# Softmax-sum spreading by transposition, one norm accumulator per half, and last products over two tiles, in a hybrid attention and FFN block

## The chip, the cores and the metric

The kernel runs on one core of a Trainium2 chip. The metric is device microseconds of one execution. It took 1214.15 us before the change, the median of 3 runs between 1213.70 and 1214.68. Less is better.

## The reference

One layer over 1024 frames of width 1024, in fp32: an RMS norm, one combined projection, two groups of eight heads (softmax attention in a band, group A; stick-breaking attention, group B), an RMS norm of each group, one output projection with residual, an RMS norm, a gated FFN with a causal convolution of width 3 and residual, and a last RMS norm.

```
h = rmsnorm(x, norm1_g);  qa, ka, va, qb, kb, vb = split(h @ w_in)
ya = chunked_attention(qa, ka, va, rel_bias)   # p = softmax(qk/8 + bias), band of 9 chunks of 64
yb = stick_breaking_attention(qb, kb, vb)
x = x + concat(rmsnorm(ya, norm_a_g), rmsnorm(yb, norm_b_g)) @ w_out
u = conv3(rmsnorm(x, norm2_g) @ w_ffn_in) + conv_b;  gate, val = split(u)   # 2816 each
x = x + (silu(gate) * val) @ w_ffn_out
return rmsnorm(x, final_g)
```

## The kernel before

**Layout.** Activations lie transposed: a tile holds 128 features on the partitions and frames along the row, and `x2` is eight such tiles. A half is 512 frames (index `g`), a block is 128 frames. Products with full precision are split in high and low parts, three matmuls (fp32r) for one product; the softmax work, the transpositions and the sums of norms are plain fp32, and one such matmul may show as several records in the trace.

**Stages**, by time in the trace: projections to about 200 us; group B's attention to 341; group A's attention, 341 to 498; group A's part of the output projection (`pa`, eight feature tiles d for half 0 and then half 1), 510 to 559; with it, and into the first FFN products, the second norm; the FFN's up-projection with convolution, to about 990; its down-projection, to 1177; the last products (`last_down`) with the final norm and the output, to the end.

**Group A.** Four pairs of heads p, eight blocks i of 128 queries each. Of a block and head (h = 0, 1), TensorE makes the scores `sa` (L1058, L1059); VectorE adds the bias and takes the row maximum (L1074, L1077); ScalarE makes the exponentials `pa` with their row sums (L1086), which lie in columns 2 and 3 of the small tile `st` (`sta` in the trace); VectorE writes the reciprocals to columns 4 and 5 (`self.scale`). `turn` has TensorE transpose `pa` (`tpa`, L1111) and ScalarE copy the result to `pta` (L1115). `spread` (L1121) brings the reciprocals into the layout of the output: 64 rows of the PSUM bank `yy` hold the reciprocal sums of head 0, 64 those of head 1, for 128 queries along the row; it takes two matmuls of a column broadcast to 64 columns with the identity. `output` (L1137) then makes the attention products beside it. Blocks go through `spread` and `output` in pairs, so there are 16 such places. A planner, `flow`, holds an estimate of each engine's clock and puts matmuls of the output projection (`k_p`, `pb`) between this work as filler; `flow.need(x)` fills until x is estimated to be done.

**The second norm.** For a half, `norm_part` has ScalarE square each x2 tile as it is finished; the first square starts an accumulator, those of d = 1 to 6 go through `sq` and an addition on GpSimd (L1680), and that of d = 7 is written straight into a second accumulator (L1674). `totals` (L168) sums the partitions of the accumulators, with four matmuls of two output columns per accumulator, into `n_ms`; a root and a reciprocal follow (L160, L161), the spreading across partitions (`n_rb`, L181), and for each feature tile a multiplication on VectorE (L1699), a copy to the high part on ScalarE, and the low part on VectorE (L129). Half 0's norm is stepped beside half 1's `pa`, a step after each d by `(1, 1, 1, 1, 1, 1, 1, 2)`, the first step being the sums and the root. Half 1's begins in `up_first`, after five products of `up_first` (`plain`, L1919, three matmuls each).

**The end.** `last_down` works on three chunks of columns: frame blocks 0 to 2, 3 to 5, and 6 to 7. For a tile d, TensorE makes the product, VectorE adds it to x2 (L2291), ScalarE squares it (in the last chunk the squares of d = 5, 6, 7 go straight into accumulators of their own, the others through GpSimd). `final` then makes the root, `n_rb`, a copy `n_rbs` of it in SBUF for GpSimd, and the outputs. In the last chunk VectorE makes six outputs with x2, the gain as a scalar and `n_rb` (L2266); for d = 2 and 4 ScalarE has applied the gain ahead (L2295) and GpSimd multiplies with `n_rbs` (L2264). Four DMAs of two tiles each follow on SyncE's queue (L2305).

**Constants.** `cst` is one tile of 216 columns (gains, convolution weights, a bias column), fetched at the start on ScalarE's DMA queue (L116).

## Time and profile before

| What | Value |
|---|---|
| median of 3 runs | 1214.15 us |
| the profiled execution, its own time | 1214.94 us |
| span of the trace in it | 1213.2 us |
| TensorE matmuls busy (PE) | 99% of the span |
| VectorE busy (DVE) | 77% |
| ScalarE busy (ACT) | 56% |
| GpSimd busy (POOL) | 13% |

The span is 1.74 us shorter than the execution that it belongs to, which is what lies around it. In rows of a timeline the columns are the start in us, the duration in us, the engine, the line, the operation, the tiles (out, then in), for PE the size of the weights, the shape and type, and the number of records run together; a last bracket names the wait ahead and who ended it. Matmul records overlap (the next begins before the last has ended), so a rate is read from starts, not from the sum of durations.

### The profile page before, as it was taken

How to read it: one execution, taken by the hardware profiler on the slowest of the kernel's cores; microseconds unless marked ns; L12 is line 12 of the kernel's file. 1: busy time of each engine (PE TensorE's matmuls, PEld its weight loads, DVE VectorE, ACT ScalarE, POOL GpSimd, SP SyncE). 2: the span in 40 equal slices, each digit the busy share in tenths (PEclk: the TensorE clock that was granted, in tenths of full speed). 3: DMA queues.
4: the chain of work that ended last, by engine and by line, in shares of the span. 5: the costliest groups of instructions: out<-in, count | busy, mean ns of one | idle time of the engine just before them, and what ended most of it. 6: DMA issues, size and time to landing. Idle time of an engine off the chain costs nothing.

```text
span 1213.2 us, 17233 instructions
## 1 busy us (share of the span) xinstructions
PE 1195.3 (99%) x6364; PEld 989.3 (82%) x6364; DVE 928.4 (77%) x1385; ACT 676.6 (56%) x1214; POOL 158.9 (13%) x162
## 2 busy tenths in 40 slices
PE   9999999999999999999999999999999999999997
PEld 6788888888878778788878888888888888888887
DVE  7957649878756677459997767777677779969896
ACT  7865336766666566334674555545555455444424
POOL 0001031102211111142000000000000023042036
PEclk9999999999999999999999999999999999999998
DMA  9468677877478841143033122231322196420003
GB/s 333 131 208 267 184 229 206 218 173 197 136 190 249 218 120 57 36 137 124 32 107 105 65 92 84 73 101 59 101 75 82 60 370 264 174 105 1 1 1 139
DMA packets 73650, 166.93 MB, mean 138 GB/s; under 512 B 7639, under 2 KB 23127, under 8 KB 73566
## 3 DMA queue, kind: packets, MB, share of 16 engines
q1 hardware_dynamic: 73422, 165.72, 43.0%
q8 instruction: 50, 0.82, 0.3%
q14 instruction: 34, 0.28, 0.1%
q10 hardware_dynamic: 144, 0.11, 0.0%
HBM read 118.60 MB, written 47.20 MB: 137 GB/s over the span
## 4 chain that ended last, share of the span: by engine, by line
PE 89%; DVE 5%; ACT 2%; DMA 2%; issue 1%; POOL 0%; SPq 0%; DVEq 0%; ACTq 0%; POOLq 0%
PE u_c L1867 9%; PE u_e L1867 9%; PE u_a L1867 9%; PE dz L2366 8%; PE u_b L1867 5%; PE dj L2366 4%; PE dm L2366 4%; PE v_x L503 4%; PE pa L151 3%; PE k_p L151 3%; PE v_y L503 3%; PE yb L1008 3%; PE tpb L994 3%; PE q_p L151 3%; PE yy L1137 2%; PE tpa L1111 2%
## 5 line engine op out<-in xcount | busy, mean ns | idle before, releaser
L967 DVE TENSOR_TENSOR_SCAN acts<-zb,first 128x128 f32<-128x128 f32 (+7 forms) x64 | 86.4, 1351 | 18.5 <-ACT zb L976 18.3
L1891 DVE SCALAR_TENSOR_TENSOR vt<-cv,cst,vt 128x1023 f32<-128x1023 f32 (+1 forms) x44 | 57.3, 1302 | 2.2 <-ACT vt L1885 1.4
L1891 DVE SCALAR_TENSOR_TENSOR gt<-cg,cst,gt 128x1023 f32<-128x1023 f32 (+1 forms) x44 | 56.3, 1281 | 0.9
L1086 ACT ACTIVATE pa<-sa,sta 128x640 f32<-128x640 f32 (+4 forms) x64 | 42.8, 670 | 23.3 <-DVE sta L1077 16.9
L976 ACT ACTIVATE zb<-zb 128x128 f32<-128x128 f32 (+7 forms) x64 | 40.9, 640 | 26.4 <-PE zb L959 26.4
L129 POOL TENSOR_TENSOR dx_0wl<-dr,dx_0wh 128x512 fp32r<-128x512 f32 x1 | 1.5, 1462 | 413.5 <-PE u_b L1867 413.5
L1885 ACT ACTIVATE gt<-cg,cst 128x1024 f32<-128x1024 f32 x22 | 27.4, 1244 | 36.7 <-DVE cg L1759 36.6
L998 ACT COPY tb<-tpb 128x128 f32<-128x128 f32 (+3 forms) x96 | 43.0, 484 | 6.1 <-PE tpb L994 5.3
L1115 ACT COPY pta<-tpa 128x512 f32<-128x512 f32 (+3 forms) x80 | 36.7, 483 | 16.7 <-PE tpa L1111 14.7
L994 PE MATMUL tpb<-ident,acts 128*128 128x128 f32 x288 | 43.2, 277 | 0.0
L1077 DVE TENSOR_REDUCE sta<-sa 128x1 f32<-128x640 f32 (+4 forms) x64 | 41.7, 655 | 1.3
L1756 DVE TENSOR_TENSOR up_r<-up_r 128x512 f32<-128x512 f32 x60 | 41.2, 686 | 0.8
L1111 PE MATMUL tpa<-ident,pa 128*128 128x128 f32 x240 | 38.0, 277 | 1.0 <-ACT pta L1115 0.8
L994 PEld LDWEIGHTS tpb<-ident,acts 128*128 128x128 f32 x288 | 33.1, 140 | 6.3 <-issue 2.6
L1074 DVE TENSOR_TENSOR sa<-sa,bias 128x256 f32<-128x256 f32 (+1 forms) x64 | 26.3, 413 | 12.4 <-PE sa L1059 10.2
L1111 PEld LDWEIGHTS tpa<-ident,pa 128*128 128x128 f32 x240 | 27.9, 140 | 8.1 <-issue 2.6
L2054 ACT COPY u_b<-u_a 128x512 f32<-128x512 f32 x19 | 10.8, 571 | 38.1 <-PE u_a L1867 38.1
L1008 PE MATMUL yb<-tb,dv 128*64 128x128 f32 x448 | 29.2, 273 | 0.0
L151 PE MATMUL pb<-yh,wo_h 128*128 128x512 f32 x64 | 27.3, 426 | 1.7 <-DVE x L1212 1.7
L1756 DVE TENSOR_TENSOR dr<-dr,dr 128x512 f32<-128x512 f32 x40 | 28.8, 740 | 0.0
L1137 PE MATMUL yy<-pta,v 128*64 128x256 f32 (+1 forms) x288 | 28.7, 344 | 0.0
L1900 DVE TENSOR_TENSOR vt<-vt,gt 128x1024 f32<-128x1024 f32 x22 | 26.8, 1218 | 1.2 <-ACT gt L1897 1.1
(1395 smaller groups left out, 4000.8 us busy)
## 6 DMA issues: line engine op xcount, KB each, us to landing
up_r<-in_w_up_dram SPq DMA_DIRECT2D x44, 512.0 KB, 3.6
act<-vt SPq DMA_DIRECT2D x22, 512.0 KB, 2.6
dr<-in_w_dn_dram SPq DMA_DIRECT2D x20, 512.0 KB, 6.8
dr<-act SPq DMA_DIRECT2D x20, 512.0 KB, 6.9
wv<-in_w_v_dram SPq DMA_DIRECT2D x16, 256.0 KB, 5.4
xin<-in_xT_dram SPq DMA_DIRECT2D x16, 256.0 KB, 5.4
row<-in_x_rows_dram SPq DMA_DIRECT2D x16, 256.0 KB, 2.7
raw<-in_w_in_dram SPq DMA_DIRECT2D x8, 512.0 KB, 5.1
```

What stands on the lines that cost most here:

```text
L151: PE.matmul(o, w[:, sl], t[:, rows(g)], start=first and i == 0, stop=last and i == 2,)
L503: PE.matmul(bank[j], t[:, cols(j)], w, start=p in (1, 5) and k == 0 and i == 0, stop=k == 3 and i == 2, skip_group_check=True,)
L967: V.tensor_tensor_scan(out=a[:, :w], data0=z, data1=first[:, :w], initial=1.0, op0=ALU.mult, op1=ALU.max,)
L994: PE.transpose(tp[:, cols(b)], self.a[h][:, cols(b0 + b)], ident)
L998: mine.append(flow.add(on_s(m * P, lambda o=o, tp=tp: S.copy(o, tp))))
L1008: PE.matmul(yy[HS[h], :], (d if j else v)[:, off : off + 64], self.at[h][:, self.c0[h] + j * P : self.c0[h] + (j + 1) * P], start=j == 0, ...
L1111: PE.transpose(tp[:, cols(b)], self.pr[src][:, cols(c)], ident)
L1137: PE.matmul(yy[HS[h], q], v[:, c * P + h * 64 : c * P + (h + 1) * 64], t[:, h], start=j == 0, stop=j == len(parts) - 1, skip_group_check=True,
L1756: eng.tensor_tensor(out=out, in0=a, in1=b, op=ALU.subtract)
L1867: PE.matmul(o, w[:, cols(k)], t, start=start and k == 0 and i == 0, stop=k == 3 and i == 2, skip_group_check=True,)
L1891: V.scalar_tensor_tensor(out=t[:, : T - lag], in0=o[:, lag:], scalar=c1(c + ct), in1=t[:, : T - lag], op0=ALU.mult, op1=ALU.add,)
L2366: PE.matmul(o[m], w[:, cols(m)], t, start=i in (0, 1, 4, 5) and p == ps_[0] and j == 0, stop=p == ps_[-1] and j == 2, skip_group_check=True,)
```

## The change

**Group A.** In `turn` of head 1, ScalarE copies the two reciprocals of a block, each broadcast to 64 columns, to a tile of 128 by 128 (`sh`, one tile of two blocks, one buffer). `spread` transposes that tile into `yy`, one transposition for a block instead of two matmuls, and waits for the copy instead of the reciprocals.

```
-                flow.need(self.scale)
-                for h in range(2):
-                    PE.matmul(
-                        rr[HS[h], :], self.st[:, 4 + h : 5 + h].to_broadcast([P, 64]), ident,
-                        start=True, stop=True, skip_group_check=True,
-                    )
+                o, wide = self.share
+                flow.need(wide)
+                PE.transpose(rr, o.rearrange("p h c -> p (h c)"), ident)
...
+                if h:
+                    if not odd:
+                        shares[self.p] = pools["sbuf"].tile([P, 2, 2, 64], F32, tag="sh", name=f"sh{nm}", bufs=1)
+                    o, share = shares[self.p][:, odd], self.st[:, 4:6].rearrange("p (h c) -> p h c", c=1)
+                    self.share = o, flow.add(
+                        on_s(P, lambda o=o: S.copy(o, share.to_broadcast([P, 2, 64]))), after=[self.scale]
+                    )
```

On TensorE, at the first spread after 350 us (head pair 0, blocks 2 and 3), before:

```order
L1059 MATMUL sa_5_0_4201<-la_3589,qa_3440 128x384
L1121 MATMUL yy_3_4206<-ident,sta_2_0_4024 64x128 x2
L1121 MATMUL yy_3_4206<-ident,sta_3_0_4076 64x128 x2
L1137 MATMUL yy_3_4206<-pta_2_4102,v_2960 64x256 x8
L1137 MATMUL yy_3_4206<-pta_2_4102,v_2960 64x128 x4
L1111 MATMUL tpa_4_0_4233<-ident,pa_4_0_4163 128x128 x4
```

and in the changed kernel:

```order
L1062 MATMUL sa_5_0_4208<-la_3592,qa_3440 128x384
L1131 MATMUL yy_3_4214<-ident,sha_2_4129 128x128 x2
L1144 MATMUL yy_3_4214<-pta_2_4110,v_2960 64x256 x8
L1144 MATMUL yy_3_4214<-pta_2_4110,v_2960 64x128 x4
L1121 MATMUL tpa_4_0_4239<-ident,pa_4_0_4168 128x128 x4
```

Four matmuls with 64 columns of weights have become two with 128, in the same place; the neighbours are the same.

**The second norm.** Each half has one accumulator: the square of d = 7 too goes through `sq` and the addition on GpSimd, and `totals` takes four matmuls instead of eight. Half 0's norm is stepped by `(0, 1, 1, 1, 1, 1, 2, 2)`, one `pa` later, and half 1's sums stand behind six products of `up_first` instead of five.

```
-        accs = {0: [acc0[:, rows(i)] for i in range(2)]}
+        accs = {0: [acc0[:, rows(0)]]}
...
-                accs[1] = [at1[:, rows(i)] for i in range(2)]
+                accs[1] = [at1[:, rows(0)]]
...
-                for _ in range((0, (1, 1, 1, 1, 1, 1, 1, 2)[d])[g]):
+                for _ in range((0, (0, 1, 1, 1, 1, 1, 2, 2)[d])[g]):
...
-                    if n == 5:
+                    if n == 6:
                         next(norms[1])
```

On VectorE, where half 1's last `pa` tiles are added to x (L1208 and L1212, now L1215 and L1219) beside half 0's norm (L1699, now L1706; low parts L129, now L132), before:

```order
L1208 TENSOR_TENSOR pa_1_5711<-pa_1_5711,rba 128x512
L1212 TENSOR_TENSOR x_6_5268<-x_6_5268,pa_1_5711 128x512
L1699 SCALAR_TENSOR_TENSOR x_5_4925<-x_5_4925,cst,n_0_rb 128x512
L129 TENSOR_TENSOR h2l_5707<-x_4_4924,h2h_5706 128x512
L1208 TENSOR_TENSOR pa_1_5735<-pa_1_5735,rba 128x512
L1212 TENSOR_TENSOR x_7_5269<-x_7_5269,pa_1_5735 128x512
L1699 SCALAR_TENSOR_TENSOR x_6_5268<-x_6_5268,cst,n_0_rb 128x512
L129 TENSOR_TENSOR h2l_5731<-x_5_4925,h2h_5730 128x512
L1699 SCALAR_TENSOR_TENSOR x_7_5269<-x_7_5269,cst,n_0_rb 128x512
```

and in the changed kernel:

```order
L1215 TENSOR_TENSOR pa_1_5720<-pa_1_5720,rba 128x512
L1219 TENSOR_TENSOR x_6_5290<-x_6_5290,pa_1_5720 128x512
L1706 SCALAR_TENSOR_TENSOR x_4_4938<-x_4_4938,cst,n_0_rb 128x512
L132 TENSOR_TENSOR h2l_5716<-x_3_4519,h2h_5715 128x512
L1706 SCALAR_TENSOR_TENSOR x_5_4939<-x_5_4939,cst,n_0_rb 128x512
L132 TENSOR_TENSOR h2l_5740<-x_4_4938,h2h_5739 128x512
L1215 TENSOR_TENSOR pa_1_5749<-pa_1_5749,rba 128x512
L1219 TENSOR_TENSOR x_7_5291<-x_7_5291,pa_1_5749 128x512
L1706 SCALAR_TENSOR_TENSOR x_6_5290<-x_6_5290,cst,n_0_rb 128x512
```

Half 0's tile 5 has its norm multiplication two instructions later, and its low part two behind that; the last rows are the same in both.

**The end.** In the last chunk the sums x2 are written into the output tiles `res` (four feature tiles each), ScalarE applies the final gain to all eight, and the last multiplications go over two tiles at a time: three on VectorE (with `n_rb` broadcast over both) and one on GpSimd (tiles 2 and 3), each followed by its DMA.

```
+ENDS = ((0, 0), (4, 0), (2, 1), (6, 0))
...
+                if c_end == KT:
+                    for a, g in ENDS:
+                        y = res[a // 4][:, a % 4 : a % 4 + 2, :]
+                        f = (rb if g else ob).rearrange("p (o t) -> p o t", o=1).to_broadcast([P, 2, n])
+                        (GP if g else V).tensor_tensor(out=y, in0=y, in1=f, op=ALU.mult)
+                        nc.sync.dma_start(outT[a : a + 2, :, sl].rearrange("d p t -> p d t"), y)
+                    return
...
+            def gain(d):
+                y = res[d // 4][:, d % 4, :]
+                S.activation(y, y, AF.Copy, scale=c1(C_GF + d))
...
+                    if c_end == KT:
+                        if d < 4:
+                            gain(d)
```

(The calls of `gain` for d = 4 to 7 stand behind the root in the code; the scheduler puts the instructions where the rows below have them.) On ScalarE, from the root of the second chunk (`n_3_ms`) to that of the last (`n_6_ms`), before:

```order
L160 ACTIVATE rn_78<-n_3_ms,eps 128x3
L2295 ACTIVATE x2n_9047<-x2n_9047,cst 128x256
L2258 COPY n_3_rbs<-n_3_rb 128x384
L1679 ACTIVATE n_sq_10635<-x2n_9048 128x256
L1679 ACTIVATE n_sq_10634<-x2n_9049 128x256
L2295 ACTIVATE x2n_9049<-x2n_9049,cst 128x256
L1674 ACTIVATE n_acc_10629<-x2n_9050 128x256
L1674 ACTIVATE n_acc_10630<-x2n_9051 128x256
L1674 ACTIVATE n_acc_10631<-x2n_9052 128x256
L160 ACTIVATE rn_78<-n_6_ms,eps 128x2
```

and in the changed kernel, from two instructions ahead of the first root and without its last four rows ahead of the second:

```order
L1686 ACTIVATE n_sq_10648<-res_10646 128x256
L2293 ACTIVATE res_10646<-res_10646,cst 128x256
L163 ACTIVATE rn_78<-n_3_ms,eps 128x3
L2293 ACTIVATE res_10646<-res_10646,cst 128x256
L1686 ACTIVATE n_sq_10649<-res_10646 128x256
L2270 COPY n_3_rbs<-n_3_rb 128x384
L2293 ACTIVATE res_10646<-res_10646,cst 128x256
L1686 ACTIVATE n_sq_10648<-res_10647 128x256
L2293 ACTIVATE res_10647<-res_10647,cst 128x256
L1681 ACTIVATE n_acc_10643<-res_10647 128x256
L2293 ACTIVATE res_10647<-res_10647,cst 128x256
L1681 ACTIVATE n_acc_10644<-res_10647 128x256
```

Each square is now followed by a gain of its tile, and two gains stand ahead of the first root.

**Constants.** `cst` holds 40 columns; the 176 columns of the convolution are a tile of their own, fetched on SyncE's queue in `up_first`, behind the weights of up-projection tile 1 and ahead of those of tile 2.

```
-    cst = one("cst", "cst", shape=(P, C_N))
-    nc.scalar.dma_start(cst, consts[:, :C_N])
+    cst = one("cst", "cst", shape=(P, C_W0))
+    nc.scalar.dma_start(cst, consts[:, :C_W0])
...
+            nc.sync.dma_start(conv["t"], consts[:, C_W0:C_N])
             load_up(2)
```

More of the change, by code (lines that the diff above doesn't have):

```diff
@@ L35 @@
 ORDER_B = (7, 0, 6, 1, 5, 2, 4, 3)
-POOL_D = {3: (2,), 6: (6, 7), 8: (2, 4)}
+POOL_D = {3: (2,), 6: (6, 7)}
+ENDS = ((0, 0), (4, 0), (2, 1), (6, 0))
 BACK, BACK_STEP = 1.0, 0.6
@@ L56 @@
 H2_TAGS = {0: ("x6", "x7"), 1: ("x0", "x1"), 2: ("x2", "x3")}
-C_G1, C_G2, C_GY, C_GF, C_W0, C_W1, C_W2, C_CB, C_TB = 0, 8, 16, 24, 32, 76, 120, 164, 208
+C_G1, C_G2, C_GY, C_GF, C_TB, C_W0, C_W1, C_W2, C_CB = 0, 8, 16, 24, 32, 40, 84, 128, 172
 C_N = 216
@@ L113, in one @@
         return pool.tile(list(shape), dt, tag=tag, name=name)
-    cst = one("cst", "cst", shape=(P, C_N))
-    nc.scalar.dma_start(cst, consts[:, :C_N])
+    cst = one("cst", "cst", shape=(P, C_W0))
+    nc.scalar.dma_start(cst, consts[:, :C_W0])
+    conv = {}
     def c1(off):
-        return cst[:, off : off + 1]
+        t, off = (cst, off) if off < C_W0 else (conv["t"], off - C_W0)
+        return t[:, off : off + 1]
     ident = one("ident", "ident", shape=(P, P))
@@ L1142, in output @@
                 flow.work(0.15)
-        pts, x2, yh, yl, yb_of, yq_of, bias_of = {}, {}, {}, {}, {}, {}, {}
+        shares, pts, x2, yh, yl, yb_of, yq_of, bias_of = {}, {}, {}, {}, {}, {}, {}, {}
         rb_of, sq_of, y_chains, x2_chains, yb_chains = {}, {}, {}, {}, {}
@@ L1749, in tile_hybrid_block @@
         fp = pools["sbuf"]
+        conv["t"] = fp.tile([P, C_N - C_W0], F32, tag="conv", name="conv", bufs=1)
         def at(slot, name, dt=F32):
@@ L2252, in final @@
                 rstd([a[:, sl] for a in last], c0, c_end, D, rn2, f"n3_{c0}")
+                if c_end == KT:
+                    for d in range(4, KT):
+                        gain(d)
                 yield
@@ L2258, in final @@
                 S.copy(rb, ob)
+                if c_end == KT:
[5 more added lines that the diff above has]
+                    return
                 pool_d = POOL_D[c_end]
                 for d in range(KT) if c_end == 6 else sorted(range(KT), key=lambda d: d not in pool_d):
-                    x = x2[d][:, sl]
-                    y = res[d // 4][:, d % 4, :] if c_end == KT else x
+                    x = y = x2[d][:, sl]
                     if d in pool_d:
@@ L2268, in final @@
                         )
-                    if c_end < KT:
-                        nc.sync.dma_start(outT[d][:, sl], y)
+                    nc.sync.dma_start(outT[d][:, sl], y)
                     if d not in pool_d:
                         yield
+            def gain(d):
+                y = res[d // 4][:, d % 4, :]
+                S.activation(y, y, AF.Copy, scale=c1(C_GF + d))
             def go(steps):
@@ L2290, in last_down @@
                             )
-                    V.tensor_tensor(out=x2[d][:, sl], in0=x2[d][:, sl], in1=o, op=ALU.add)
+                    y = x2[d][:, sl] if c_end < KT else res[d // 4][:, d % 4, :]
+                    V.tensor_tensor(out=y, in0=x2[d][:, sl], in1=o, op=ALU.add)
                     last = accs[: {3: 1, 6: 2, 8: 4}[c_end]]
-                    x2_part(x2, d, sl, [a[:, sl] for a in last], None, f"n3_{c0}", sqs[d % 2][:, :GW])
-                    if d in POOL_D[c_end]:
+                    x2_part({d: y}, d, slice(0, y.shape[1]), [a[:, sl] for a in last], None, f"n3_{c0}", sqs[d % 2][:, :GW])
+                    if c_end == KT:
+                        if d < 4:
+                            gain(d)
+                    elif d in POOL_D[c_end]:
                         S.activation(x2[d][:, sl], x2[d][:, sl], AF.Copy, scale=c1(C_GF + d))
@@ L2303, in last_down @@
             go(20)
-            for i in range(4):
-                nc.sync.dma_start(
-                    outT[2 * i : 2 * i + 2, :, sl].rearrange("d p t -> p d t"),
-                    res[i // 2][:, 2 * (i % 2) : 2 * (i % 2) + 2, :],
-                )
         done = up_second(up_first())
@@ L2413, in _layout @@
             cols(a("norm1_g")[0]), cols(a("norm2_g")[0]), cols(a("norm_a_g")[0]),
-            cols(a("norm_b_g")[0]), cols(a("final_g")), cols(conv_w[0]), cols(conv_w[1]),
-            cols(conv_w[2]), cols(a("conv_b")[0]), np.broadcast_to(rel[:, -1], (P, 8)),
+            cols(a("norm_b_g")[0]), cols(a("final_g")), np.broadcast_to(rel[:, -1], (P, 8)),
+            cols(conv_w[0]), cols(conv_w[1]), cols(conv_w[2]), cols(a("conv_b")[0]),
             np.zeros((P, GW), np.float32),
```

## The prediction

> **What bounds the kernel.** I read the page's span and engine line first, then its chain, then the waits of TensorE, and only then the three places that the change touches.
>
> ```profile
> span 1213.2 us, 17233 instructions
> PE 1195.3 (99%) x6364; PEld 989.3 (82%) x6364; DVE 928.4 (77%) x1385; ACT 676.6 (56%) x1214; POOL 158.9 (13%) x162
> PE 89%; DVE 5%; ACT 2%; DMA 2%; issue 1%; POOL 0%; SPq 0%; DVEq 0%; ACTq 0%; POOLq 0%
> ```
>
> TensorE is busy for 99% of the span and holds 89% of the chain that ends last. So a matmul taken out is worth its slot unless the next one then waits for its data; and the 11% of the chain on other engines is where a saving can be lost. The waits (engine, line and tile, who released it: us in total, times, the longest) say where PE stands still already in group A, its output projection and the end:
>
> ```profile
> PE na_rb L181 <- DVE rn L1167: 2.2, 1, 2.2
> PE pb L151 <- DVE x L1212: 1.7, 1, 1.7
> PE sa L1058 <- ACT pa L1086: 1.3, 2, 1.2
> PE tpa L1111 <- ACT pta L1115: 0.8, 1, 0.8
> ```
>
> All of these together are 6.0 us. The kernel has little slack to give and little to lose, so the change is a sum of microseconds. The profiled execution took 1214.94 us, of which 1213.2 are the span and 1.74 lie around it; the median of the runs is 0.79 lower, so I apply the sum to the median. A difference of 0.2% (2.4 us) is about what a measurement of this kernel can tell from no change: faster means below 1211.7, slower above 1216.6.
>
> **Group A, what is removed.** The spread's records as a group, then in order of time at one pair of blocks early in the stage and at the last:
>
> ```profile
> L1121 PE MATMUL yy<-ident,sta x128: 272/273/323, 352.1 to 494.7; 128*64 128x128 f32 x128
> 352.14 0.66 PE L1121 MATMUL yy<-ident,sta 128*64 128x128 f32 x8
> 352.63 2.33 PE L1137 MATMUL yy<-pta,v 128*64 128x256 f32 x24
> 355.97 0.60 PE L1111 MATMUL tpa<-ident,pa 128*128 128x128 f32 x4
> 494.13 0.27 PE L1111 MATMUL tpa<-ident,pa 128*128 128x128 f32 x1
> 494.33 0.66 PE L1121 MATMUL yy<-ident,sta 128*64 128x128 f32 x8
> ```
>
> The group has 128 records, 8 at each of 16 pairs. From the start of the 8 to the start of what follows are 352.63 − 352.14 = 0.49 us. In place of them come two transpositions with 128 columns, of the kind of `tpa`: four of those take 0.60 and one 0.27, so a further one costs (0.60 − 0.27)/3 = 0.11, and two take 0.22. That saves 0.27 a pair. A part may stay: after a transposition the 64-column records start 494.33 − 494.13 = 0.20 later instead of 0.11, a change of shape that the new kernel has too, in front of L1137 instead; half of that 0.09, 0.05, I charge to each pair. So the saving is between 0.22 and 0.27, and 16 pairs give 3.5 to 4.3 us; I take 3.9, all on PE's path.
>
> The Trainium skill, "TensorE: Matmul & The Clock Gate", section Terms, says that on trn2 matmul has a transpose mode that is four times faster for fp32. By it the pair would cost an estimated 0.12 us in place of 0.49, and 16 pairs would save 5.9; the trace's own transpositions, 0.11 apart, make it 2.2 times.
>
> **Group A, what is added.** ScalarE gets 32 copies of 128 by 128 with a broadcast source. No row has a broadcast source; the nearest is the smallest copy of `tpa`, the first row. Then come the last `pta` copy and the products after it at the pair where they lie closest, and the stage as a whole (time, then busy time of PE, its weight loads, DVE, ACT, POOL, then granted clock, DMA share, GB/s):
>
> ```profile
> L1115 ACT COPY pta<-tpa 128x128 f32<-128x128 f32 x8 | 2.1, 264 | 2.4 <-PE tpa L1111 2.4
> 479.33 0.85 ACT L1115 COPY pta<-tpa 128x512 f32<-128x512 f32 x2
> 480.52 1.68 PE L1137 MATMUL yy<-pta,v 128*64 128x256 f32 x14
> 341.00:498.00 157.00, 153.61 (x1116) 124.19 (x1117) 104.31 (x254) 100.63 (x250) 19.04 (x28) 1.00 0.52 150
> ```
>
> 32 copies at 0.2 (the part in which the next instruction can't run, by my estimate from the row's 0.264) are 6.4 us, and ACT goes from 100.6 to some 107 busy of 157. Behind each copy on ACT stand the `pta` copy and the next exponentials, for which PE waits at `tpa` and `sa`: the two rows of waits on ACT above, 2.1 us in three waits. Elsewhere ACT is ahead of PE: the two rows of about 480 us are the tightest of the pairs, and there the products L1137 start 0.34 us after the end of the last `pta` copy that they read (480.52 − (479.33 + 0.85)); in the other pairs it is over 0.75. A copy of 0.2 fits in. The cost lies between 0 and 6.4 (every copy on the path). At the three waits two or three copies fall in the span that PE waits for; with some places left where ACT is only just ahead I take +1.0, nearer the low end, since the row is nearest to a hidden copy. VectorE does nothing new. The release of 1.7 by DVE (`pb` <- x) follows from PE's own product through DVE and back, with the order unchanged, and stays. Group A: −3.9 + 1.0 = **−2.9**, from −4.3 to +2.9.
>
> **The second norm.** Both sums, and what follows each:
>
> ```profile
> 537.37 1.84 PE L168 MATMUL n_ms<-ones,n_acc 128*128 128x2 f32 x16
> 539.08 0.49 PE L151 MATMUL pa<-yh,wo_h 128*128 128x512 f32 x1
> 559.33 0.39 PE L1919 MATMUL u<-h2h,up_wh 128*128 128x512 f32 x1
> 562.73 1.84 PE L168 MATMUL n_ms<-ones,n_at 128*128 128x2 f32 x16
> 564.43 0.49 PE L1919 MATMUL u<-h2h,up_wh 128*128 128x512 f32 x1
> ```
>
> 539.08 − 537.37 = 1.71 and 564.43 − 562.73 = 1.70 for 16 records: half of them, 8, take 0.85 each, and the sum would be −1.7. But at both ends of this stretch other engines are next in line:
>
> ```profile
> 545.00:564.70 19.70, 19.48 (x94) 16.08 (x93) 19.36 (x29) 9.68 (x16) 8.78 (x6) 1.00 0.35 121
> 562.02 0.68 DVE L129 TENSOR_TENSOR h2l<-x,h2h 128x512 fp32r<-128x512 f32 x1
> 563.28 1.46 DVE L129 TENSOR_TENSOR h2l<-x,h2h 128x512 fp32r<-128x512 f32 x2
> 561.48 0.64 ACT L1674 ACTIVATE n_at<-x 128x512 f32<-128x512 f32 x1 [1.31 <-DVE x L1212]
> 559.66 1.61 POOL L1680 TENSOR_TENSOR n_at<-n_at,n_sq 128x512 f32<-128x512 f32 x1 [0.98 <-ACT n_sq L1679]
> ```
>
> From 545 to 564.7 DVE is busy for 19.36 of 19.70 us (the window's third figure), and its work there is the same after the change, so its last low parts come at 564.74 (563.28 + 1.46) whatever PE saved. Its last five rows are in the old order, so the low part of tile 5 is ready at some 562.02 + 0.6 = 562.6. PE, ahead by the 0.85 of the first sum, reaches the products at 558.5 instead of 559.33, does five (0.68 each, three matmuls at (562.73 − 559.33)/15 = 0.227) until 561.9, and waits some 0.7 us for that part; if it is further ahead, it waits longer, to the same time. Next, the sums of half 1 now stand behind the sixth product, and wait for GpSimd: the last square ends at 561.48 + 0.64 = 562.12, and instead of being in an accumulator it needs the addition, 1.61, until 563.7. The sixth product ends near 563.1, so another 0.6 is waited; 8 records until 564.6, the seventh product to 565.3. Before, the eighth product began at 564.43 + 6 × 0.227 = 565.8. So **−0.5** of the −1.7 stays. The bounds: −1.7 if DVE and GpSimd run earlier by as much as PE, +0.5 if the last addition starts 0.98 later, the wait of POOL for ACT in its row.
>
> What a wait of that size can do beyond itself is in the windows around the wait of 2.2 at `na_rb`:
>
> ```profile
> 510.20:513.70 3.50, 3.40 (x13) 3.10 (x14) 0.00 (x0) 1.17 (x2) 1.01 (x2) 0.51 0.39 110
> ```
>
> After an idle of 2.2 us the granted clock was 0.51 for 3.5 us, and cost half of it, 1.7; the idle of 1.7 at `pb` left it at 1.00. My two new waits, 0.7 and 0.6 with a product between them, lie below. This 1.7 exists before and after alike.
>
> The Trainium skill, "TensorE: Matmul & The Clock Gate", section Part 1: The HAM clock gate, gives about 3.4 us of idle, a whole window of a free-running counter, as what halves the clock. Here 2.2 us were enough, so the trace is stricter than the page; by the page neither wait could cost more than itself.
>
> **The end.** ScalarE, PE, VectorE and the DMA issue in the last chunk, then the DMA windows:
>
> ```profile
> 1199.30 0.26 ACT L160 ACTIVATE rn<-n_ms,eps 128x3 f32<-128x3 f32 x1
> 1199.46 0.50 ACT L2295 ACTIVATE x2n<-x2n,cst 128x256 f32<-128x256 f32 x1
> 1203.76 0.42 ACT L1674 ACTIVATE n_acc<-x2n 128x256 f32<-128x256 f32 x1 [0.19 <-DVE x2n L2291]
> 1203.35 1.95 PE L168 MATMUL n_ms<-ones,n_acc 128*128 128x2 f32 x16
> 1205.33 0.26 ACT L160 ACTIVATE rn<-n_ms,eps 128x2 f32<-128x2 f32 x1 [1.15 <-PE n_ms L168]
> 1206.78 2.44 DVE L2266 SCALAR_TENSOR_TENSOR res<-x2n,cst,n_rb 128x256 f32<-128x256 f32 x6 [0.47 <-ACT n_rbs L2258]
> 1207.67 1.99 SPq L2305 DMA_DIRECT2D out_dram<-res  x4
> 1205.00:1208.25 3.25, 0.72 (x5) 0.40 (x4) 2.45 (x7) 0.63 (x2) 1.62 (x3) 0.73 0.98 352
> 1208.50:1211.75 3.25, 0.00 (x0) 0.00 (x0) 0.71 (x2) 0.00 (x0) 0.00 (x0) 0.50 0.96 323
> ```
>
> The multiplications themselves change little: six at 2.44/6 = 0.41 become three over twice the columns, some 0.6 to 0.8 each; the last DMA issue is not what ends the kernel, since the DMA engines are busy at 0.96 to 0.98 from 1205 until 1211.75 with the outputs. What moves is when the last megabyte can start. ACT now does six more gains of 0.5 (some 0.4 where they run close). Two stand ahead of the second chunk's root, which goes from 1199.30 to about 1200.0, and the multiplications and outputs of that chunk with it; the later ones stand ahead of the squares: with three gains more ahead of the last square it comes at about 1205.3 instead of 1203.76. The sums of the last chunk then end at 1206.4 instead of 1205.3, one pass of DVE's first multiplication starts at 1207.8 instead of 1206.78, and the first output DMA is issued at about 1208.5 instead of 1207.67. The transfers lose the same, in part: the queues still have outputs of the second chunk then, also later. I take **+0.8**; the bounds are −0.2 (gains all beside waits, and the passes as short as they can be) and +1.5 (the whole delay of the last square).
>
> **The constants.** At the start `cst` is shorter, and the convolution's columns, fetched beside the weights of tile 1, are first read only after products with those weights:
>
> ```profile
> L116 ACTq DMA_DIRECT2D cst<-in_consts_dram x1: 397/397/397, 0.8 to 0.8; - x1
> DMA to landing us min/median/max: 2.9/2.9/2.9
> 4.62 0.72 ACT L309 ACTIVATE hTh<-xin,cst 128x512 fp32r<-128x512 f32 x1 [2.10 <-DMA xin<-in_xT_dram]
> ```
>
> It lands at 0.8 + 2.9 = 3.7, before its first reader at 4.6, which waits for another DMA, so less of it is worth **−0.1** (0 to −0.3). On SyncE the new issue stands ahead of tile 2's weights, 0.09 MB in front of 0.5; nothing waits.
>
> **The rivals.**
>
> (1) *The whole saving.* ACT hides every copy, DVE and POOL shift with PE, the gains fall into waits: −3.9 − 1.7 − 0.2 − 0.1 = −5.9, **1208.25**. For it: ACT is 64% busy in group A. Against it: DVE's unbroken rows in the norm.
>
> (2) *Group A's saving becomes waits.* The filler is set by estimates, and PE, faster by 0.25 a pair, finds ACT's exponentials and `pta` copies 0.2 later: a wait of the same size replaces the records, −3.9 + 3.9, and the rest −0.5 + 0.8 − 0.1 = +0.2: **1214.3**. For it: the two waits on ACT that exist. Against it: 0.34 and more of lead at the products.
>
> (3) *The clock gives way.* The waits in the second norm run together to 2.2 us, because the addition on POOL comes 0.6 to 1.0 later than I think; then the clock halves as it did at 510.20, +1.7, and the wait itself +0.5: −2.7 + 2.2 = −0.5, **1213.7**.
>
> (4) *Slower.* Each of the 32 copies stands in ACT's queue ahead of a `pta` copy or an exponential for which PE is waiting: 32 × 0.2 = +6.4 against −3.9 makes +2.5, and with the +0.2 of the rest +2.7: **1216.9**. It decides where ACT's lead over PE is under 0.2 us at most spreads. The leads of 0.34 and more speak against it.
>
> (5) *Faster transpositions.* If a pair's two transpositions took a quarter of the 0.49 that they replace, 0.12, the 16 pairs would save 5.9 instead of 3.9: −2.7 − 2.0 = −4.7, **1209.4**. The rows of `tpa`, 0.11 for each, speak against it. It is the skill's rule on fp32 transpositions, named above.
>
> **How the numbers follow.** −2.9 − 0.5 + 0.8 − 0.1 = −2.7; on the profiled execution 1214.94 − 2.7 = 1212.2, on the median 1214.15 − 2.7 = 1211.45; I say **1211.4**. Chances: the forecast, within a microsecond or so, 0.45; rival (1) 0.17; (5) 0.03; (2) 0.17; (3) 0.12; (4) 0.06. The forecast stands at the bound of what can be told, 1211.7, so its chance is split 0.28 to 0.17: faster 0.28 + 0.17 + 0.03 = 0.48; the same 0.17 + 0.17 + 0.12 − 0.01 = 0.45; slower 0.06 and 0.01 from the far end of (2), 0.07. The range goes from (1) to past (2), by the 0.7 by which the end may cost more than I take: 1208.2 to 1215.0. Left out are (4) and the outer halves of (1) and (2), less than 0.2 in all.
>
> **What would show it.** Group A: 32 records of `yy`<-`sh` 0.11 apart and the stretch from 341 to 498 shorter by about 3; waits of `tpa` and `sa` on ACT that grow from 2.1 to no more than 3.5; if they reach 6, (2) or (4). The norm: `n_ms` with 8 records in 0.85, a wait of about 0.6 in front of the second, released by POOL, one of 0.7 or more before a product `u`, released by DVE, and a granted clock of 1.00 behind them; 0.5 there is (3). The end: the root of the second chunk 0.7 later against the product before it, the first issue of the last four DMAs 0.9 later, and the end of transfers 0.8 later. What would make it wrong most easily: a copy with a broadcast source that takes far longer than 0.264, or the filler falling differently around the pairs.

## The result, and the profile after

The changed kernel takes 1218.18 us (median of 7 runs, 1217.34 to 1219.68), the kernel before 1214.15 (7 runs): a ratio of 1.0033, with a 95% interval from 1.0022 to 1.0045. It is slower, by 4.0 us, and outside the range that was given. The profiled execution took 1217.90.

The first lines of the page, and its chain, after:

```profile
span 1216.2 us, 17043 instructions
PE 1195.9 (98%) x6252; PEld 984.3 (81%) x6252; DVE 927.5 (76%) x1382; ACT 685.3 (56%) x1252; POOL 161.9 (13%) x163
PE 88%; DVE 6%; ACT 3%; DMA 1%; issue 1%; POOL 0%; SPq 0%; DVEq 0%; ACTq 0%
```

TensorE executes 112 records fewer (6252 for 6364) and is busy 0.6 us longer. So something made the records that remain longer, and the waits cannot tell what; these are TensorE's, after:

```profile
PE pb L154 <- DVE x L1219: 1.8, 1, 1.8
PE na_rb L184 <- DVE rn L1174: 1.7, 1, 1.7
PE sa L1061 <- ACT pa L1089: 1.7, 3, 1.2
PE u L1928 <- DVE h2l L132: 1.4, 1, 1.4
PE tpa L1121 <- ACT pta L1125: 1.1, 2, 0.8
PE n_ms L171 <- POOL n_at L1687: 0.4, 1, 0.4
PE nb_rb L184 <- ACT pta L1125: 0.2, 1, 0.2
```

They are much as forecast: some 0.8 more behind ScalarE at `sa`, `tpa` and `nb_rb` together, and the two new ones of the norm (1.4 and 0.4). The time must be found by place. One way is to take the same instruction in both traces and compare its start. From TensorE's timeline before, the end of group A (an output projection product just behind the last `yy`), the norm, the end of the down-projection, and the last `n_rb`:

```profile
496.63 0.50 PE L151 MATMUL pb<-yh,wo_h 128*128 128x512 f32 x1
567.07 0.39 PE L1919 MATMUL u<-h2h,up_wl 128*128 128x512 f32 x1
1177.29 2.96 PE L2287 MATMUL dnl<-lx,lw 128*128 128x384 f32 x16
1205.85 0.43 PE L181 MATMUL n_rb<-ident,rn 128*128 128x128 f32 x2 [0.55 <-DVE rn L161]
```

and after:

```profile
493.74 0.40 PE L154 MATMUL pb<-yh,wo_h 128*128 128x512 f32 x1
563.97 0.47 PE L1928 MATMUL u<-h2h,up_wl 128*128 128x512 f32 x1
1179.36 2.94 PE L2308 MATMUL dnl<-lx,lw 128*128 128x384 f32 x16
1208.94 0.43 PE L184 MATMUL n_rb<-ident,rn 128*128 128x128 f32 x2 [0.55 <-DVE rn L164]
```

The changed kernel is 2.9 ahead at the end of group A, still 3.1 ahead at 567 us, and 2.1 behind at the start of the last products. It loses 5.2 us between, in the FFN, where the change alters nothing except where the convolution's constants lie. The end adds 1.0, to the 3.0 by which the spans differ.

In the FFN there is no new wait. The loss grows evenly: by 0.15 us in every 15 from 620 to 980 us, and by 0.10 in the down-projection. One window of 390 us in both, columns as in the prediction (before, then after):

```profile
600.00:990.00 390.00, 389.56 (x1718) 321.96 (x1717) 299.37 (x359) 221.15 (x324) 5.71 (x4) 1.00 0.29 98
```

```profile
600.00:990.00 390.00, 389.82 (x1703) 319.17 (x1702) 296.05 (x354) 217.95 (x319) 5.24 (x4) 1.00 0.28 97
```

At the same granted clock of 1.00, and as busy, TensorE gets through 1703 matmuls instead of 1718: 229 ns each instead of 227. The view of one tile shows that the records themselves are longer (minimum, median and maximum in ns, then first and last start), before and after:

```profile
L1867 PE MATMUL u_e<-h2h,us_7ph x8: 389/389/389, 704.0 to 716.9; 128*128 128x512 f32 x8
```

```profile
L1875 PE MATMUL u_e<-h2h,us_7ph x8: 392/393/394, 701.9 to 715.0; 128*128 128x512 f32 x8
```

Before, every one of the eight takes 389. After, none does. A matmul that takes 3 to 5 ns longer at full clock, in a pattern that repeats for each tile, is hardly one that waits for another engine. What the change altered for it is the place of its operands.

**Where the operands lie.** `cst` shrank from 864 to 160 bytes in each partition, and all long-lived tiles behind it moved down by 704. The tiles of the FFN stage lie above them, and first among them is now the convolution's tile, of 704 bytes: so these stayed where they were. Addresses in the built programs, in bytes:

```
                                   before   after
h2h (k = 0), moving, long-lived    110208   109504
us_8ph, weights, FFN stage         171648   171648
difference, modulo 256                  0      192
```

Before, all 2712 fp32r matmuls of the FFN with 512 columns have their two operands a multiple of 256 bytes apart. After, 1080 have not (1008 lie 192 off, 72 lie 64). My theory: **a matmul of this kind is slower when its weights and its moving operand do not lie a multiple of 256 bytes apart**, and the next ones suffer too until the cadence is found again (the other 1632 after are slowed in part). The rivals: the constants' own tile, its DMA or its readers cost the time; the other parts of the change cost it; the address itself, not the distance, counts.

### The profile page after: what moved, and what is told of

Read it like the earlier page. It is cut to its first block, busy times and chain, and to the rows that moved or that the text cites. A ratio compares the mean times of both kernels' runs of the same rounds, so it can differ in the third digit from the quotient of the medians.

```text
span 1216.2 us, 17043 instructions
## 1 busy us (share of the span) xinstructions
PE 1195.9 (98%) x6252; PEld 984.3 (81%) x6252; DVE 927.5 (76%) x1382; ACT 685.3 (56%) x1252; POOL 161.9 (13%) x163
## 4 chain that ended last, share of the span: by engine, by line
PE 88%; DVE 6%; ACT 3%; DMA 1%; issue 1%; POOL 0%; SPq 0%; DVEq 0%; ACTq 0%
PE u_c L1875 9%; PE u_a L1875 9%; PE u_e L1875 9%; PE dz L2386 8%; PE u_b L1875 5%; PE dm L2386 4%; PE dj L2386 4%; PE v_x L506 4%; PE pb L154 3%; PE pa L154 3%; PE k_p L154 3%; PE v_y L506 3%; PE yb L1011 3%; PE tpb L997 3%; PE q_p L154 3%; PE yy L1144 2%
## 5 line engine op out<-in xcount | busy, mean ns | idle before, releaser
L1899 DVE SCALAR_TENSOR_TENSOR vt<-cv,conv,vt 128x1023 f32<-128x1023 f32 (+1 forms) x44 | 58.3, 1325 | 2.2 <-ACT vt L1893 1.5
L1899 DVE SCALAR_TENSOR_TENSOR gt<-cg,conv,gt 128x1023 f32<-128x1023 f32 (+1 forms) x44 | 57.4, 1305 | 1.5 <-ACT gt L1893 0.7
L132 POOL TENSOR_TENSOR dx_0wl<-dr,dx_0wh 128x512 fp32r<-128x512 f32 x1 | 1.4, 1357 | 414.6 <-ACT dx_0wh L2142 414.6
L1893 ACT ACTIVATE gt<-cg,conv 128x1024 f32<-128x1024 f32 x22 | 27.4, 1244 | 39.9 <-DVE cg L1767 39.8
L1687 POOL TENSOR_TENSOR n_acc<-n_acc,n_sq 128x384 f32<-128x384 f32 (+2 forms) x24 | 25.6, 1065 | 28.9 <-ACT n_sq L1686 28.1
```

The source lines that it names most:

```text
L1899: V.scalar_tensor_tensor(out=t[:, : T - lag], in0=o[:, lag:], scalar=c1(c + ct), in1=t[:, : T - lag], op0=ALU.mult, op1=ALU.add,)
```

## The experiments

In all of these "before" is the kernel before, timed on the same chip: 1214.84 us in the first set of four, 1214.72 in the second, 1214.46 in the third, 1214.50 for the last.

### The FFN's tiles moved back (after_al)

The changed kernel, with the convolution's tile 16 columns wider:

```
-        conv["t"] = fp.tile([P, C_N - C_W0], F32, tag="conv", name="conv", bufs=1)
+        conv["t"] = fp.tile([P, 192], F32, tag="conv", name="conv", bufs=1)
...
-            nc.sync.dma_start(conv["t"], consts[:, C_W0:C_N])
+            nc.sync.dma_start(conv["t"][:, : C_N - C_W0], consts[:, C_W0:C_N])
```

> The changed kernel with one number altered: the tile of the convolution constants is 192 columns (768 bytes) wide instead of 176 (704), so that the tiles of the FFN stage lie a multiple of 256 bytes from where they lay relative to the long-lived tiles before the change. Theory (place of the operands): the matmuls from 567 us to 1177 us go back from a mean of 229 ns to 226.7, which gives back the 5.0 us lost there; the gain of about 3 us ahead of them and the loss of about 1 us at the end stay, so about 1212.1 us. Rival 1 (reading or fetching the constants from a tile of their own costs the time): no change, 1218. Rival 2 (the lost time came with the parts in groups A, the norm and the end): no change, 1218.

Measured: 1213.24 us (11 runs, 1211.10 to 1215.70), 0.9987 of before (0.9978 to 0.9996). 64 unused bytes took 4.9 us away. The row of `us_8ph`, the tile of the addresses above (its matmuls take 392 to 394 in the changed kernel), and the window:

```profile
L1875 PE MATMUL u_e<-h2h,us_8ph x8: 389/389/390, 718.6 to 731.5; 128*128 128x512 f32 x8
600.00:990.00 390.00, 389.16 (x1716) 321.36 (x1715) 299.71 (x356) 218.81 (x319) 7.02 (x5) 1.00 0.30 102
```

The matmuls are back at 389 and at 1716 in the window. The constants are still in a tile of their own, fetched by their own DMA and read by the same instructions, so the first rival falls; so does the second, since all other parts of the change are there.

### The constants' split alone (before_const)

The kernel before, with the constants in two tiles as in the change (the order of the columns and `c1` too):

```
-    cst = one("cst", "cst", shape=(P, C_N))
+    cst = one("cst", "cst", shape=(P, C_W0))
...
+        conv["t"] = fp.tile([P, C_N - C_W0], F32, tag="conv", name="conv", bufs=1)
```

> The kernel before with only the constants split in two tiles as in the change. Theory: the FFN's tiles move by 704 bytes against the long-lived ones, not a multiple of 256; matmuls of 229 ns, +5.0 us there, -0.3 at the start, so about 1219. Rival 1 (the constants' own reading or fetching) gives the same here, and differs in the run above. Rival 2 (the other parts of the change): 1214.

Measured: 1219.78 us (4 runs), 1.0045 (1.0030 to 1.0060), 4.9 slower than before. This part alone makes more than the whole loss of the change, and its window holds 1702 matmuls, where the changed kernel's holds 1703:

```profile
600.00:990.00 390.00, 389.80 (x1702) 319.19 (x1701) 296.16 (x355) 217.26 (x318) 4.46 (x3) 1.00 0.28 95
```

### A gap of 128 bytes in the kernel before (before_ffn128)

An unused tile stands ahead of the FFN stage's tiles:

```
         fp = pools["sbuf"]
+        fp.tile([P, 32], F32, tag="gap", name="gap", bufs=1)
```

> The kernel before with an unused tile of 128 bytes ahead of the FFN stage's tiles; nothing else. Theory with a period of 256 bytes: matmuls whose weights and moving tile differ by 128 bytes are as slow as the products at the start of the kernel that differ so (mean 232 ns there against 227.8), about half of the FFN's, so +5 us or more: 1219 to 1221. Theory with a period of 128 bytes: 1214. Rival 1 (constants): 1214.

Measured: 1223.21 us (4 runs), 1.0067 (1.0054 to 1.0081). An unused tile costs 8.4 us. Nothing else is changed, so no instruction, DMA or constant can be the cause, and the period is not 128 bytes. The cost is larger than for 192 (8.4 against 4.9), and larger than I expected. The view of the tile and the window:

```profile
L1868 PE MATMUL u_e<-h2h,us_7ph x8: 392/394/405, 705.9 to 719.1; 128*128 128x512 f32 x8
600.00:990.00 390.00, 390.00 (x1689) 316.92 (x1688) 293.89 (x355) 216.04 (x316) 2.60 (x2) 1.00 0.26 90
```

### All tiles moved together (before_all64)

The first tile is 64 bytes wider:

```
-    cst = one("cst", "cst", shape=(P, C_N))
-    nc.scalar.dma_start(cst, consts[:, :C_N])
+    cst = one("cst", "cst", shape=(P, C_N + 16))
+    nc.scalar.dma_start(cst[:, :C_N], consts[:, :C_N])
```

> The kernel before with the first tile 64 bytes wider, so that all tiles move by 64 bytes together. Theory (only the distance between the two operands counts): 1214, matmuls of the FFN at 226.7 ns. Rival (the address itself must be a multiple of 128 bytes): all matmuls slower, 1219 or more.

Measured: 1214.24 us (10 runs), 0.9997 (0.9988 to 1.0006): no change, with 1718 matmuls in the window. Each address moved by 64 bytes, the distances stayed: the distance counts. The third rival falls, as far as a move of 64 bytes can show it.

### The parts of the change, each undone on the mended base (al_noA, al_noB, al_noC)

With the FFN's tiles in place, each other part can be taken back by itself. The base is after_al, 1213.24, which was timed in the first set (the kernel before differs by 0.1 between the two). In al_noA `spread` uses the two matmuls of before, and ScalarE's copies are gone:

```
-                PE.transpose(rr, o.rearrange("p h c -> p (h c)"), ident)
+                for h in range(2):
+                    PE.matmul(
+                        rr[HS[h], :], self.st[:, 4 + h : 5 + h].to_broadcast([P, 64]), ident,
...
```

> The changed kernel with its FFN tiles back at a multiple of 256 bytes (1213.2 in the run before), and the spreading of the softmax sums as before the change. Theory (the forecast's term for group A, 2.9, which the trace of that run reads as 2.6): slower by that, 1215.8. Rival (waits on ScalarE take the whole saving): 1213.2.

Measured: 1217.55 us (7 runs), 1.0028 (1.0017 to 1.0039): 4.3 slower than the base. The transposition is worth it, and by more than its trace says. Aligned start by start, the base is 2.5 ahead of this run at the end of group A. The rest comes later: this run's trace has a halved clock from 563 to 569.8 us, in the norm, which the base's has not. The mean granted clock of each run tells how far that goes for the others: six of the seven runs lie at 0.994 or 0.995 (1217.3 to 1218.4 us), four of the base's eleven do (1213.2 to 1215.7). At equal clock the transposition is worth some 3 us, as forecast; the rest of the 4.3 is clock.

In al_noB the second norm is as before:

```
-        accs = {0: [acc0[:, rows(0)]]}
+        accs = {0: [acc0[:, rows(i)] for i in range(2)]}
...
-                accs[1] = [at1[:, rows(0)]]
+                accs[1] = [at1[:, rows(i)] for i in range(2)]
...
-                for _ in range((0, (0, 1, 1, 1, 1, 1, 2, 2)[d])[g]):
+                for _ in range((0, (1, 1, 1, 1, 1, 1, 1, 2)[d])[g]):
...
-                    if n == 6:
+                    if n == 5:
```

> The same base, the second norm as before the change. Theory (0.5 of the nominal 1.7 is kept, the rest becomes waits on VectorE and GpSimd): slower by 0.5, 1213.7. Rival 1 (all of it kept): 1214.9. Rival 2 (the new waits cost more than the sums, with a halved clock behind them in part of the runs): faster, 1212 to 1213.

Measured: 1210.78 us (9 runs, 1210.46 to 1211.92), 0.9973 (0.9963 to 0.9982): **2.5 faster** without the norm's part, and with runs within 1.5 us of each other where the base's lie within 4.6. My theory of 0.5 kept falls; rival 2 stands, and goes further than the 1212 to 1213 that it named. The mean granted clock of the runs bears it out: the base's three runs at 0.998 take 1211.1 to 1211.7 us, its other eight, at 0.994 to 0.997, 1212.4 to 1215.7, and no run of al_noB lies under 0.996. At 0.998 the two kernels are only 0.6 apart. What the new waits do is in the windows around them, first of the changed kernel, then of al_noB:

```profile
557.00:560.40 3.40, 1.64 (x10) 1.06 (x9) 3.40 (x6) 1.84 (x3) 1.60 (x1) 1.00 0.65 188
560.40:564.00 3.60, 3.60 (x12) 2.83 (x12) 1.81 (x4) 1.99 (x4) 0.00 (x0) 0.54 1.02 395
```

```profile
557.00:560.40 3.40, 3.40 (x25) 3.11 (x24) 3.11 (x6) 1.89 (x4) 0.00 (x0) 1.00 0.79 231
```

In the changed kernel TensorE is busy for 1.64 of 3.40 us, and in the 3.6 after it the granted clock is 0.54: matmuls every 0.42 to 0.44 us instead of 0.23 (TensorE's timeline, after):

```profile
559.64 1.05 PE L171 MATMUL n_ms<-ones,n_at 128*128 128x2 f32 x8 [0.41 <-POOL n_at L1687]
560.55 0.64 PE L1928 MATMUL u<-h2h,up_wh 128*128 128x512 f32 x1
560.99 0.63 PE L1928 MATMUL u<-h2l,up_wh 128*128 128x512 f32 x1
```

In al_noC the last chunk is as before (the function `final` and the last products as in the kernel before, with their gains inside the six multiplications on VectorE).

> The same base, the last chunk as before the change (six multiplications with the gain inside on VectorE, two on GpSimd, four DMAs behind them). Theory (the gains on ScalarE make roots, sums and the first output DMA later by 0.8 to 1.1): faster by that, 1212.3. Rival (the end is set by the transfers alone): 1213.2.

Measured: 1211.89 us (11 runs, 1210.23 to 1214.07), 0.9982 (0.9973 to 0.9991): 1.35 faster than the base by the medians. Both scatter over some 4 us, and their intervals overlap, so the runs alone do not show that the last part costs what was expected; the trace, further below, has 0.9.

### The early stages' tiles too (al_st_noC, before_st)

The same rule finds 368 matmuls of the kernel before whose operands lie 128 bytes apart: products of the projections and of the output projection, because four small tiles of 32 bytes each lie below the tiles of the early stages. (16 more lie 192 apart, and are still off after the edit.) Made 64 bytes each:

```
-                    self.st = kp.tile([P, 6], F32, tag="st", name=f"st{nm}", bufs=4)
+                    self.st = kp.tile([P, 16], F32, tag="st", name=f"st{nm}", bufs=4)
```

> The same base, the last chunk as before the change, and the small tile of the softmax sums 64 bytes wide instead of 24 (four buffers: 256 bytes instead of 128), which moves the tiles of the stages before the FFN by 128 bytes against the long-lived ones. The 368 matmuls of the projections and the output projection whose two operands lie 128 bytes apart, of a mean of 232 ns, then lie at a multiple of 256. Theory: 368 x 5 ns = 1.9, and some 0.4 where their disturbance runs on into the next ones: 1212.3 - 2.3 = 1210.0. Rival (the early stages are slow for another reason, their transfers): 1212.3.

> The kernel before, with the small tile of the softmax sums 64 bytes wide instead of 24 and nothing else: the tiles of the early stages move by 128 bytes, and 368 matmuls have their operands a multiple of 256 bytes apart. Theory: 1214.7 - 1.8 to 2.3 = 1212.4 to 1212.9, the projections' products at a mean near 227 ns instead of 231. Rival (the early products are slow because of their transfers): 1214.7.

Measured: al_st_noC 1210.10 us (6 runs), 0.9964 (0.9952 to 0.9976), 1.8 faster than al_noC by the medians (the intervals overlap a little); before_st 1212.60 (11 runs), 0.9981 (0.9972 to 0.9990), 1.9 faster than the kernel before, by forty bytes more in each of four small tiles, which nothing reads. One group of the projections, in the kernel before and in before_st:

```profile
L1248 PE MATMUL ee<-t,s x48: 390/393/404, 99.2 to 159.9; 128*128 128x512 f32 x48
```

```profile
L1248 PE MATMUL ee<-t,s x48: 389/389/390, 98.9 to 158.6; 128*128 128x512 f32 x48
```

These matmuls run beside heavy transfers (a DMA share of 0.7), which I had offered as a rival cause. They are at 389 as soon as the distance is right. The kernel before by itself says the same: of its products of 512 columns ahead of 200 us, those whose operands and whose successor's weights lie right (362) have a mean of 227.9 ns to the next start (gaps of over 0.26 us left out), those where neither does (293) 232.4, in the same stretch and beside the same transfers. This also speaks against a rival that moving the tiles does not exclude, that accesses of other engines to the moved tiles slow TensorE.

### What is best, and which half of the norm costs (best, best_half1, best_half0)

best is al_st_noC with the second norm as before. best_half1 has the norm's change for half 1 alone, best_half0 for half 0 alone:

```
-                accs[1] = [at1[:, rows(0)]]
+                accs[1] = [at1[:, rows(i)] for i in range(2)]
...
-                    if n == 6:
+                    if n == 5:
```

(the edit that makes best_half0 from al_st_noC; best_half1 takes the other two edits of al_noB.)

> The spreading by transposition alone of the change (with the constants split, which makes room for its tile), the second norm and the last chunk as before the change, and all large tiles a multiple of 256 bytes apart. Theory: 1210.8 (the run without the norm's part) - 1.35 (the last chunk's part) - 1.8 to 2.3 (the early stages' tiles) = 1207.1 to 1207.6, and a granted clock of 1.00 from 550 to 570 us. Rival (the gains of the runs overlap, since each also shifts where the clock halves): 1208.5 or more.

> The kernel above with the norm's change for half 1 alone (one accumulator, four matmuls, its sums behind the sixth product); half 0's accumulators and steps as before the change. Theory (half 0's steps, one tile later, make the low parts late, and that wait halves the clock): no wait on VectorE before the products u, no halved clock, 0.85 saved less a wait of 0.4 on GpSimd: 0.4 faster than the kernel above, 1206.9. Rival (half 1's wait for GpSimd is what halves the clock): 1.5 to 3 slower than the kernel above, 1209 to 1210.

> The spreading by transposition, the split constants and all large tiles a multiple of 256 bytes apart as in the run called best; of the norm, the change for half 0 alone (one accumulator, its steps one tile later), half 1 as before the change; the last chunk as before the change. Theory (half 0's later steps make the low parts late, and the wait for them halves the clock): a wait on VectorE before a product u or beside the sums, a halved clock near 560, 1.5 to 2.5 slower than best (1208.05): 1209.5 to 1210.5. Rival (it takes both halves: with five products and 16 records of sums ahead, the low part comes in time): within 0.5 of best, 1207.2 to 1208.5.

Measured: best 1208.05 us (5 runs, 1207.76 to 1208.43), **0.9944** of before (0.9932 to 0.9957), 10.1 us under the changed kernel's median; best_half1 1207.90 (1207.62 to 1208.00), 0.9943, the same within what can be told; best_half0 1209.95 (1207.89 to 1211.19), 0.9955 (0.9941 to 0.9969).

So half 1's part is harmless. Half 0's costs time in a part of the runs: its median is 1.9 higher, two of its five runs are as fast as those of best (1207.89, 1208.32), and they scatter over 3.3 us where the other two scatter over 0.7 and 0.4. The way is not quite the one I expected. The trace of best_half0 shows no wait for a low part before a product `u`. It shows the 16 sums of half 1 torn in two by a short wait for the last square, and a halved clock behind them. Its windows, then TensorE's timeline:

```profile
556.10:559.50 3.40, 3.23 (x23) 2.77 (x23) 3.31 (x6) 2.01 (x4) 0.00 (x0) 1.00 0.39 110
559.50:562.95 3.45, 3.45 (x10) 2.69 (x10) 0.99 (x3) 0.99 (x3) 0.00 (x0) 0.54 0.95 340
```

```profile
556.38 0.95 PE L170 MATMUL n_ms<-ones,n_at 128*128 128x2 f32 x8
557.50 1.05 PE L170 MATMUL n_ms<-ones,n_at 128*128 128x2 f32 x8 [0.17 <-ACT n_at L1680]
558.41 0.48 PE L1927 MATMUL u<-h2h,up_wh 128*128 128x512 f32 x1
```

The sums, matmuls of two columns, take 2.0 us here (556.38 to 558.41) and TensorE counts as busy in them; yet the clock halves. In best they take 1.7 in one piece, and no stretch around them was below 1.00.

## Why the prediction was wrong

**The step that failed** is the constants: "less of it is worth −0.1 (0 to −0.3)" and "nothing waits". The gain at the start is not shown either: the projections' products stand 0.2 us earlier in the changed kernel's trace, and 0.1 and 0.4 later in those of after_al and before_const, which have the same shorter `cst`. The step counted instructions, DMAs and waits, and the cost is in none of them: it was 4.9 us, by before_const and by after_al alike, because the split put 1080 of the FFN's matmuls at a distance that is not a multiple of 256 bytes. A tile whose size changes moves every tile behind it, and this was not looked at. It was not among the rivals either; the rival that came out slower, a copy on ScalarE ahead of each wait, did not happen.

Without that step the time is 1218.18 − 4.9 = 1213.3, and after_al measured 1213.24: inside the range, 1.8 above the 1211.4 that was given. That it lies so near is partly luck. By the medians group A saved 1.4 more than its term, and the norm cost 3.0 more than its own and had the sign wrong. The terms:

- *Group A*, forecast −2.9 (−3.9 and +1.0 for ScalarE): the trace shows −2.5 against al_noA. The pair of transpositions takes 0.31 us instead of 0.49 in thirteen of the 16 places (the forecast said 0.22 to 0.27), so 2.9 are saved there in all; some 0.6 more are left over, perhaps where the filler falls otherwise (not shown). ScalarE's copies take 302 ns each, 9.7 in all. They cost what was estimated: `sa`, `tpa` and `nb_rb` wait 1.0 longer than in al_noA. So the term that was mis-sized here is the removal, 2.9 in place of 3.9. The Trainium skill, "TensorE: Matmul & The Clock Gate", section Terms, has a transpose mode that is four times faster for fp32. Here 0.49 became 0.31, 1.6 times. By the medians the part is worth 4.3. The profiled run without it had a halved clock for 6.8 us that the base's had not, which is 3.4 us; by the granted clocks above, more of its runs than of the base's had one.

```profile
L1116 ACT COPY sha<-sta 128x128 f32<-128x128 f32 x32 | 9.7, 302 | 1.0 <-DVE sta L1096 1.0
351.85 0.38 PE L1131 MATMUL yy<-ident,sha 128*128 128x128 f32 x2
352.16 2.38 PE L1144 MATMUL yy<-pta,v 128*64 128x256 f32 x24
```

- *The second norm*, forecast −0.5, cost +2.5. The two waits came where they were put (1.4 for the low part, forecast 0.7 or more; 0.4 for GpSimd, forecast 0.6). What was wrong is "My two new waits ... lie below", the reading that 2.2 us of idle at one time are needed to halve the clock. This was rival (3), given 0.12; it happened with waits smaller than the rival asked for. The wait of 1.7 at `pb` that the reading leaned on is no bound either: it is in all fourteen profiles, and in that of before_st the clock halved behind it, as the stretch that holds it (a wait of 1.76 before 405.47) and the next one show:

```profile
402.62:406.03 3.41, 1.65 (x8) 1.10 (x7) 2.90 (x7) 1.52 (x4) 0.00 (x0) 1.00 0.93 201
406.03:409.44 3.41, 3.41 (x17) 3.18 (x15) 2.44 (x7) 2.10 (x4) 0.61 (x1) 0.50 0.45 151
```

- *The end*, forecast +0.8: 1.35 by the medians, not clear of the scatter, and in the trace 0.9 (the first output DMA of the last four is issued at 1210.59 instead of 1207.67, 2.9 later, of which 2.1 were there at the start of the last products). The mechanism, gains ahead of roots and squares, was right: the root of the second chunk is 0.7 later against the products. What it left out is that `n_rb` then waits 0.4 us behind the sums of that chunk; in after_al's trace the clock halved there for 3.4 us.

```profile
1202.06 0.24 ACT L163 ACTIVATE rn<-n_ms,eps 128x3 f32<-128x3 f32 x1
1210.59 2.09 SPq L2276 DMA_DIRECT2D out_dram<-res  x4
```

The clock also accounts for much of the spread: over the base's eleven runs the time grows by some 1 us for each 0.001 that the mean granted clock falls. Before, the halved 3.4 us behind the wait at `na_rb` are in the profile; with the transpositions that wait is 1.7 instead of 2.2 (2.1 in al_noA), and no profile with 1.7 shows a halved clock there. The changed kernel trades this place for the one in the norm.

## What to carry to other kernels

When a tile changes size, or one is added, compare the addresses of all matmul operands before and after, modulo 256: here 64 unused bytes were worth 4.9 us, more than the transposition saved (4.3). When a saving seems to vanish, compare the starts of the same instruction along the trace; a loss that grows evenly with time, at an unchanged clock and with no wait, is in the instructions themselves. And a shorter row of work on the busiest engine is only a gain where what feeds it comes earlier too; otherwise the wait can cost more than itself.

## What the runs showed of the hardware

**The distance of a matmul's operands.** For fp32r matmuls of 512 columns, the mean from start to start between 600 and 990 us (gaps of over 0.3 us left out) is 226.7 ns where all distances are multiples of 256 bytes; in the changed kernel, with 192 for about half, it is 229; with 128, 231. The records of the tiles shown above take 389, 392 to 394 and 392 to 405 ns. Within one run the disturbance does not end at once: in the changed kernel, matmuls at a right distance have a mean of 228.7 from the start before theirs, though only 40 of the 840 stand right behind one that is not. It may be that the next matmul's weights, which are loaded while a matmul runs (in the changed kernel's trace one load begins at 720.00 us beside a matmul that begins at 719.99), count as well: early in the kernel before, 40 products have their own operands right and the next one's weights 128 bytes off, and a mean of 234; 39 have it the other way round, and 232. In the FFN the two almost always go together, so the runs do not tell them apart. Tried were 128 and 192 (64 for a few matmuls only), and a move of all tiles by 64, without effect; other distances and other types were not. Why the distance matters was not found.

**The clock.** The clock halved for 3.4 us, or for 6.8, and then was full again. It did so behind 2.2 us of idle (before); behind 1.76 (before_st, at `pb`); behind 1.4 and 0.4 of idle with eight narrow sums between other products (after); and behind 2.0 us of narrow sums with 0.2 of idle (best_half0). In the seven profiles where it halved behind idle ahead of the last products, TensorE was busy for 1.3 to 1.8 us of the 3.4 us just before. It is partly chance: the wait at `na_rb` is 2.0 to 2.2 us in the profiles of six kernels, and the clock halved behind it in two of them (before, before_ffn128); it is 1.7 in eight, and halved in none. The wait at `pb`, 1.7 to 1.8 in all fourteen, halved it in one. The norm's two waits of the changed kernel are in five profiles: it halved behind them in four (after, al_noA, al_noC, al_st_noC), and not in after_al. Narrow sums of 1.7 us in one piece (al_noB, best) did not halve it. The Trainium skill, "TensorE: Matmul & The Clock Gate", section Part 1: The HAM clock gate, speaks of a free-running window of 3413 ns. The lengths of 3.4 and 6.8 us, and the chance in it, agree with this. That a whole window must be idle does not agree: the window before the halved one had TensorE busy for 1.64 of 3.40 us in one case, and for 3.23 in the other. That narrow matmuls count for little would explain the second; it was not tested by itself.
